# A two-layer decoder trunk: the last layer's output projection with tokens on the partitions, and four output tiles side by side at the start of each layer

## The chip, the cores and the metric

The kernel runs on one core of one Trainium2 chip, as a single program. The metric is the device time of one execution in microseconds (us), inputs and weights in HBM at its start and the output in HBM at its end. A core has a matrix engine (PE, with its weight loads shown apart as PEld), a vector engine (DVE), a scalar engine (ACT), GpSimd (POOL) and a queue engine that starts the transfers (SP). Each works through its own list of instructions in order and waits on semaphores for the others.

## The reference

```python
D_MODEL, SEQ, DEPTH = 1024, 256, 2      # BATCH = 1
N_HEADS, HEAD_DIM, IDX_HEADS, IDX_DIM, D_RNN = 8, 128, 16, 64, 1408
def rmsnorm(x, g):
    return x * rsqrt(mean(x * x, -1, keepdims=True) + 1e-6) * g
for l in range(DEPTH):
    h = rmsnorm(x, norm_g[l])
    q, k, v, ga, iq, ik, iw, xr, gr, ma, mb = split(h @ w_in[l])
    q, k, iq, ik = rope(q), rope(k), rope(iq), rope(ik)
    # index score I[t,s] = sum_h iw[t,h] relu(iq[t,h] . ik[s]); each query keeps its top 64 causal keys
    attn = softmax_attention(q, k, v, kept_keys)
    y_a = (attn * silu(ga)) @ w_out_attn[l]
    xr = causal_depthwise_conv(xr, conv_w[l], conv_b[l])
    y_b = (rg_lru(xr, ...) * silu(gr)) @ w_out_rnn[l]
    x = x + (sigmoid(ma) * y_a + sigmoid(mb) * y_b) @ w_o[l]
return rmsnorm(x, final_g)              # (1, 256, 1024), float32
```

## The kernel before, in words

Activations lie with features on the partitions: the residual stream x is eight tiles of 128 features x 256 tokens. All large matrix products run on PE in fp32r as three products of a high and a low part (`mm3`: high weights by high input, low by high, high by low), so each 128x128 block of weights costs three matmuls.

The weights come from HBM as one stream, `wst`, in the order of use, in chunks of eight blocks (128x1024, 512 KB). A chunk lands in one of four `raw` buffers; ACT (or DVE) copies it to `wh`, the high part, and DVE subtracts to get `wl`, the low part; there are six buffers of each. The first two chunks come in quarters instead (`raq`, 128x256, split into `wq`), so that PE can begin earlier.

`plan()` lists each layer's units in PE's order: `ik` (the index keys and head weights, one output tile `pk`, line 822), `iq` 0 to 7 (index queries, line 853), between them and after them the gates `ga`, `ma`, `mb`, the recurrent branch (`xr`, `gr`, `gate`, whose tiles are `rps` in the profile), then q, k, v and attention, `yb`, `ya` (the two branches' projections, with tokens on the partitions and 512-column matmuls, `by_token`, line 924) and `wo` (line 1156), which turns back to features on the partitions: 128x256 tiles `ops`, added to x.

Work on `ik` and `iq` does not wait for the norm: it multiplies `xg` = x times the gain (line 781, ACT for the high part, DVE for the low), and the factor R = 1/rms per token enters later, in `ci` and `si` (the rotary tables times R), in `iwt`, and in `hf` = x times gain times R (line 851), which is split into `hh` and `hl` for all other projections. `hl` is what the first `ga` matmul needs; `kh` and `kl`, the split rotated index keys, are what the index scores `dots` need.

The norm (lines 709 to 774) has three modes. "wide" (layer 0) multiplies each of eight squared tiles `nsq` with a matrix of ones on PE, at full width 128x256 and in fp32, then takes square root (ACT) and reciprocal (DVE) at 128x256. "added" (layer 1) adds the squares on DVE and needs two narrow sums (one column of output each), square root and reciprocal at 128x2, then two small matmuls `rps` (diagonal `dg` by ones) that spread R over the partitions. "columns" (after the last layer) sums each of the eight squared tiles by two narrow matmuls.

After the last layer (lines 1194 to 1203) the norm is finished, `fo` = x times the final gain (ACT), times R (DVE), and five transfers of 128 or 256 KB write the output, features on the partitions.

The order on each engine is not the order of the code. The class `Program` records every operation with a cost, its inputs and outputs and, for PE, its place in plan order (a `late` term moves it back); then it hands out buffers and picks, engine by engine, what can start earliest. PSUM has four banks with the tag `pp` (pk, iq, ga, ma, mb, ops, ...), two `pq` and two `pt` (norm sums, transposes).

Of the kernel before, what the change touches and what calls it, by code (L numbers as in the profile page):

```python
# [42 lines left out]
for _n, _w in (("g", 8 * L), ("cw", 4 * KR * L), ("cb", KR * L), ("br", KR * L), ("bi", KR * L), ("lam", KR * L),  # L43
               ("fg", 8), ("inv_a", 1), ("sgn_a", 1), ("inv_i", 1), ("sgn_i", 1)):
    PC[_n] = _c
    _c += _w
NPAR = _c

# [16 lines left out]
def plan():  # L65

    u = [("ik",)]
# [4 lines left out]
    u += iq[:NRAW]  # L72
# [19 lines left out]
    u += [("yb", n) for n in range(2)]  # L92
    u += [("ya", n) for n in range(2)]
    u += [("wo", m, 0, 4) for m in range(6)] + [("wo", m, 4, 8) for m in range(6)]
    u += [("wo", m, 0, 8) for m in range(6, 8)]
    return u
# [22 lines left out]
def unit_blocks(u):  # L119

    n = u[0]
    if n == "ik":
        return [("in80", k, OFF["ik"]) for k in range(KD)]
    if n == "attn":
        return []
# [12 lines left out]
    if n == "ya":  # L138
        return [("oa", k, u[1] * 512 + a * P) for k in range(KD) for a in range(4)]
    return [("o", k, u[1] * P) for k in range(u[2], u[3])]  # L140


NBLK = L * sum(len(unit_blocks(u)) for u in plan())
# [3 lines left out]
class H:  # L147


    def __init__(self, pool, tag, shape, dt, name, bufs):  # L150
        self.pool, self.tag, self.shape, self.dt, self.name, self.bufs = pool, tag, shape, dt, name, bufs
        self.tile = None
        self.writer = None
        self.readers = []
        self.users = 0
        self.index = None
# [71 lines left out]
class Program:  # L228
# [15 lines left out]
    def op(self, eng, cost, outs, ins, emit, tabs=ANY, alt=None):  # L244
# [12 lines left out]
        for h in ins:  # L257
            if h.writer is not None and h not in outs:
                o.preds.add(h.writer)
        for h in outs:  # L260
            if h.writer is None:
# [5 lines left out]
            else:  # L267
                o.preds.add(h.writer)
# [4 lines left out]
        for h in outs:  # L273
            h.writer = o.no
            h.readers = []
# [153 lines left out]
def trunk(ctx, tc, xT, pos, par, wst, out):  # L429
# [83 lines left out]
    def load(o, src, cost):  # L513
        pg.op("dma", cost, [o], [], lambda: nc.sync.dma_start(real(o), src))
# [8 lines left out]
    class Stream:  # L523
# [6 lines left out]
        def load(self, upto):  # L530
            while self.nload < min(upto, NCH):
                c = self.nload
                self.nload += 1
                if c < QUARTERS:
                    self.raws[c] = []
                    for i in range(4):
                        raw = f1("raq")
                        load(raw, wst[c][:, 256 * i:256 * i + 256], 400)
# [8 lines left out]
        def chunk(self, c):  # L547
            if c not in self.parts:
# [4 lines left out]
                if c < QUARTERS:  # L553
                    self.parts[c] = []
                    for q in raw:
                        t = halves(r2("wq"))
# [12 lines left out]
        def block(self, n=1):  # L569
# [4 lines left out]
            if c < QUARTERS:  # L574
                s = slice(r % 2 * P, r % 2 * P + P)
                return p[r // 2][0][:, s], p[r // 2][1][:, s]
# [18 lines left out]
    head = const("head", [NPAR + T])  # L595
    load(head, par, 500)
    prm = head[:, :NPAR]
    x = [const(f"x{k}", [T]) for k in range(KD)]
    first = ws.load(QUARTERS)
    for k in range(KD):  # L600
        if k % 2 == 0:
            next(first)
        if k > 0:
            load(x[k], xT[:, k, :], 400)
    for _ in first:
        pass
    pg.after = POS_AFTER
    posi = const("posi", [T], I32)
    load(posi, pos, 400)
    load(x[0], xT[:, 0, :], 400)  # L610
    pg.after = 0.0

    def pc(n, i=0):
        return prm[:, PC[n] + i:PC[n] + i + 1]
# [4 lines left out]
    vset(hpi, math.pi / 2)  # L619
    ones = const("ones", [P])  # L620
# [68 lines left out]
    def decay():  # L689
        lam = prm[:, PC["lam"]:PC["lam"] + NL]  # L690
# [18 lines left out]
    class Norm:  # L709


        def __init__(self, mode):
            self.mode = mode
            self.acc = None
            self.n = 0

        def sums(self, s, first, last):

            if first:
                self.ps = bank("pt", "nps")  # L720
            pg.late = LATE_SUM
            for t in range(2):
                mm(self.ps[:, 0, t:t + 1], s[:, t * P:t * P + P], ones[:, 0:1], first and t == 0, last, True, cost=213)
            pg.late = 0.0

        def all_sums(self, s, first, last):

            if first:
                self.ps = bank("pt", "nps")
            pg.late = LATE_SUM  # L730
            mm(self.ps[:, 0, :], ones, s, first, last, cost=432)
            pg.late = 0.0

        def add(self, k):
            s, xk = f1("nsq"), x[k]
            if self.mode != "added":
                pg.op("act", 94 + 0.833 * T, [s], [xk],
                      lambda: nc.scalar.activation(real(s), real(xk), AF.Square),
                      alt=(67 + 1.046 * T, lambda: nc.vector.tensor_tensor(real(s), real(xk), real(xk), op=OP.mult)))
                if self.mode == "wide":  # L740
                    self.all_sums(s, self.n == 0, self.n == KD - 1)
                else:
                    self.sums(s, self.n == 0, self.n == KD - 1)
            else:
                act(s, xk, AF.Square)
                if self.acc is None:
                    self.acc = s
                else:
                    add(self.acc, self.acc, s)
            self.n += 1  # L750

        def finish(self, copied=True):
            if self.mode == "wide":
# [540 lines left out]
```

## Time and profile before

| | us |
|---|---|
| time, median of 3 runs (lowest, highest) | 711.24 (711.12, 711.37) |
| the profiled execution | 711.33 |
| its span | 709.6 |
| PE busy | 693.7 (98%) |
| DVE busy | 598.0 (84%) |
| ACT busy | 488.8 (69%) |

The profile shows one execution of 711.33 us; its rows lie within the span of 709.6 us, so 1.7 us lie outside of it. Busy time counts an engine's executing instructions; matmuls are pipelined, so a row's mean duration of one matmul is longer than the distance at which they follow each other, and it is the distance that counts for a sum. The chain of waits is the sequence of pieces of work that ended last, followed back from the end.

### The profile page before, as it was taken

Reading aid. Unit: us, or ns where it says so; the run is one execution under the profiler, and the core shown is the slowest. Engines: PE = TensorE matmul, PEld = TensorE weight load, DVE = VectorE, ACT = ScalarE, POOL = GpSimd, SP = SyncE. Lnnn points to the kernel's source line nnn. Section 1 sums busy time; section 2 is a strip of 40 time slices with the busy share of each in tenths; the row PEclk is TensorE's granted clock in tenths of the full one; section 3 lists DMA queues with packets and bytes.
Section 4 is the critical chain, followed back from the end, with each engine's and each line's share of the span. In section 5 each row is a group of like instructions: output and inputs, shape, how many; then the busy total and the mean of one; then the engine's idle time right before and its main releaser. Section 6 shows DMA issues by size and latency. Waiting matters only on the chain.

```text
span 709.6 us, 12900 instructions
## 1 busy us (share of the span) xinstructions
PE 693.7 (98%) x4836; PEld 647.9 (91%) x4836; DVE 598.0 (84%) x1178; ACT 488.8 (69%) x794; POOL 6.4 (1%) x18
## 2 busy tenths in 40 slices
PE   7999999999999999999999999999999999999995
PEld 6988999999999998888999899999999898988895
DVE  6989999899897959857779997999979896996652
ACT  7997675899995748434679776588779674754432
POOL 0000000000000000000000000000000000000000
PEclk9999999999999999999999999999999999999998
DMA  7646556666656452655553555566656545445501
GB/s 256 209 156 209 170 191 203 200 196 217 216 175 194 149 189 76 208 179 178 178 178 113 185 184 186 176 218 207 222 198 194 184 160 176 141 146 174 184 1 61
DMA packets 39402, 124.87 MB, mean 176 GB/s; under 512 B 5036, under 2 KB 9708, under 8 KB 39340
## 3 DMA queue, kind: packets, MB, share of 16 engines
q1 hardware_dynamic: 39340, 124.05, 53.5%
q8 instruction: 38, 0.62, 0.3%
q14 instruction: 24, 0.20, 0.1%
HBM read 119.38 MB, written 1.05 MB: 170 GB/s over the span
## 4 chain that ended last, share of the span: by engine, by line
PE 82%; DVE 8%; ACT 6%; issue 2%; DMA 1%; SPq 0%; DVEq 0%; ACTq 0%
PE rps L508 15%; PE yb L508 9%; PE ops L508 7%; PE k L508 6%; PE q L508 6%; PE ma L508 6%; PE v L508 6%; PE ya L508 6%; PE gps L508 5%; PE mb L508 4%; PE ga L508 4%; DVE wl L482 2%; ACT wh L476 2%; PE lg L508 2%; PE av L508 2%
## 5 line engine op out<-in xcount | busy, mean ns | idle before, releaser
L482 DVE TENSOR_TENSOR wl<-raw,wh 128x1024 fp32r<-128x1024 f32 x223 | 271.5, 1219 | 62.6 <-ACT wh L476 61.3
L476 ACT ACTIVATE wh<-raw 128x1024 fp32r<-128x1024 f32 x199 | 210.4, 1058 | 135.8 <-PE ya L508 22.9
L508 PE MATMUL rps<-hl,wh 128*128 128x256 f32 x352 | 99.6, 283 | 0.0
L508 PE MATMUL rps<-hh,wl 128*128 128x256 f32 x352 | 99.6, 283 | 0.0
L508 PE MATMUL rps<-hh,wh 128*128 128x256 f32 x352 | 99.6, 283 | 0.0
L508 PEld LDWEIGHTS rps<-hh,wh 128*128 128x128 f32 x352 | 67.5, 192 | 0.2
L508 PEld LDWEIGHTS rps<-hh,wl 128*128 128x128 f32 x352 | 67.5, 192 | 0.2
L508 PEld LDWEIGHTS rps<-hl,wh 128*128 128x128 f32 x352 | 67.5, 192 | 0.0
L508 PE MATMUL yb<-wh,g 128*128 128x512 f32 x176 | 58.9, 396 | 0.0
L508 PE MATMUL iq<-xg,wh 128*128 128x256 f32 x240 | 44.7, 284 | 0.0
L508 PE MATMUL ya<-wh,aT 128*128 128x512 f32 x128 | 40.3, 393 | 0.0
L508 PEld LDWEIGHTS iq<-xg,wh 128*128 128x128 f32 x240 | 37.9, 192 | 0.0
L508 PEld LDWEIGHTS yb<-wh,g 128*128 128x128 f32 x176 | 32.5, 188 | 5.3
L508 PE MATMUL ga<-hl,wh 128*128 128x256 f32 x128 | 36.3, 284 | 0.7 <-DVE hl L482 0.7
L508 PE MATMUL ops<-ml,wh 128*128 128x256 f32 x128 | 36.8, 287 | 0.0
L508 PE MATMUL ops<-mh,wl 128*128 128x256 f32 x128 | 36.7, 287 | 0.0
L508 PE MATMUL ops<-mh,wh 128*128 128x256 f32 x128 | 36.6, 286 | 0.0
L508 PE MATMUL q<-hh,wl 128*128 128x256 f32 x128 | 36.4, 284 | 0.0
L508 PE MATMUL q<-hh,wh 128*128 128x256 f32 x128 | 36.3, 284 | 0.0
L508 PE MATMUL k<-hh,wl 128*128 128x256 f32 x128 | 36.3, 284 | 0.0
L508 PE MATMUL q<-hl,wh 128*128 128x256 f32 x128 | 36.2, 283 | 0.0
L508 PE MATMUL k<-hh,wh 128*128 128x256 f32 x128 | 36.2, 283 | 0.0
(232 smaller groups left out, 1980.4 us busy)
## 6 DMA issues: line engine op xcount, KB each, us to landing
raw<-in_wst_dram SPq DMA_DIRECT2D x223, 512.0 KB, 3.5
xk<-xs SPq DMA_DIRECT2D x24, 48.0 KB, 3.7
raq<-in_wst_dram SPq DMA_DIRECT2D x8, 128.0 KB
x<-in_xT_dram SPq DMA_DIRECT2D x8, 128.0 KB, 3.4
out_dram<-fo SPq DMA_DIRECT2D x3, 256.0 KB
xk<-xs SPq DMA_DIRECT2D x8, 40.0 KB
xf<-xs SPq DMA_DIRECT2D x2, 160.0 KB
xf<-xs SPq DMA_DIRECT2D x2, 144.0 KB
```

Source lines behind the costliest of these rows:

```text
L476: lambda: nc.scalar.activation(real(o), real(i), AF.Copy),
L482: lambda: nc.vector.tensor_tensor(real(o), real(a), real(b), op=op))
L508: lambda: nc.tensor.matmul(real(o), real(w), real(m), start=start, stop=stop, skip_group_check=grp))
```

## The change

It has four parts.

1. Loads. The parameters are split: the norm gains, the rotary constants and the first x tile come first (`pre`, 128x276 and x 128x256), the rest (`prm`) after the first weights. x comes in pairs of tiles (`xp`). The first two chunks of weights come in four halves (`rah`, 128x512, split into `whh` and `whl`) instead of eight quarters, with whole chunks (`raw`) between them. A one-column sine loads ACT's table at the start.
2. The start of a layer. The unit `head` replaces `ik` and `iq` 0 to 2: for each of the eight rows of weights it runs the three matmuls of four output tiles (pk, iq 0, 1 and 2), in three PSUM banks.
3. The norm. There is one mode for both layers: squares of a pair of tiles (128x512) on ACT or DVE, added on DVE, then four narrow sums, square root and reciprocal of 128x2, two `dg` and two `rps`, and an ACT copy of R. x is updated in pairs of tiles.
4. The end of the last layer. `xt` transposes x to tokens on the partitions (16 transposes on PE, 4 copies on ACT) and loads the final gain, repeated on all partitions. `wt` replaces `wo`: 96 matmuls of 128x512 instead of 192 of 128x256, tokens on the partitions; the second half of the features finishes token tile 0 first and then token tile 1. The sum of squares of a token is then along the row: ACT's Square with an accumulated output. Square root and reciprocal are 128x1, and ACT scales the first half of a row, DVE the second. Four transfers of 256 KB write the output.

```diff
-    u = [("ik",)]
+    u = [("head",)]
-    u += iq[:NRAW]
+    u += iq[3:NRAW]
     u += [("yb", n) for n in range(2)]
+    if l == L - 1:
+        return u + [("xt", 0), ("ya", 0), ("xt", 1), ("ya", 1), ("wt", 0), ("wt", 1)]
...
     class Norm:
+        def add(self, i):
+            s = f2("nsq")
+            square(s.join(), xp[i].join())          # ACT, or DVE where that is earlier
+            if self.acc is None:
+                self.acc = s
+            else:
+                add(self.acc, self.acc, s)
+        def sums(self, s):
+            self.ps = bank("pt", "nps")
             pg.late = LATE_SUM
             for t in range(2):
-                mm(self.ps[:, 0, t:t + 1], s[:, t * P:t * P + P], ones[:, 0:1], first and t == 0, last, True, cost=213)
+                for a in range(2):
+                    mm(self.ps[:, 0, t:t + 1], s[:, a, t * P:t * P + P], ones[:, 0:1], t == a == 0, a == 1, True, cost=213)
-        def all_sums(self, s, first, last):
-            mm(self.ps[:, 0, :], ones, s, first, last, cost=432)
...
-        def ik(self):
-            pk = bank("pp", "pk")
+        def head(self):
+            pk, one, two = bank("pp", "pk"), bank("pp", "iq"), bank("pp", "iq")
             ps = pk[:, 0, :]
-            proj(ps, self.xg)
             self.R = R = self.norm.finish()
+            for k in range(KD):
+                for n, o in enumerate((ps, one[:, 0, :], one[:, 1, :], two[:, 0, :])):
+                    mm3(o, self.xg[k], k == 0 and n != 2, k == KD - 1, True)
...
+        def xt(self, n):
+            for t in range(2):
+                bk = bank("pt", "xps").join()
+                for c in range(4):
+                    trans(bk[:, c * P:c * P + P], x[4 * n + c][:, t * P:t * P + P])
+                self.turned[n, t] = r2f("xt").join()
+                act(self.turned[n, t], bk, AF.Copy)
+        def wt(self, n):
+            ps = self.by_token("ops", self.m, True, True, n == 1)
+            for t in range(2):
+                y, z = self.turned[n, t], r2f("z").join()
+                add(y, y, ps[t])
+                ss = const(f"ss{n}{t}", [1])
+                act(f2("sq").join(), y, AF.Square, accum_out=ss)
+                mul(z, y, self.fg[n])
+                if n == 0:
+                    tsc(ss, ss, 1.0 / D, EPS, OP.mult, OP.add)
+                else:
+                    act(ss, ss, AF.Sqrt, scale=1.0 / D, bias=self.ss[t])
+                    recip(ss, ss)
+                    act(o, o, AF.Copy, scale=ss)
+                    tsc(z, z, ss, None, OP.mult)
+                    ...
-    R = norm.finish(False)
-    for w in (1, 2, 2, 2, 1):
-        act(o[:, a, :], x[n + a], AF.Copy, scale=pc("fg", n + a))
-        mul(o, o, R.twice()[:, :w, :])
```

Three places show how the instructions stand. On PE, the start of the program, before (pk is the index key tile, iq the index queries, nps the norm's sums):

```order
L508 MATMUL nps35_114<-nsq34_107,ones21_83 128x256
L508 MATMUL pk64_130<-xg33_105,wq65_111 128x256 x3
L508 MATMUL pk64_130<-xg36_118,wq65_111 128x256 x3
L508 MATMUL nps35_114<-nsq37_135,ones21_83 128x256
L508 MATMUL pk64_130<-xg38_123,wq66_128 128x256 x3
L508 MATMUL nps35_114<-nsq39_147,ones21_83 128x256
L508 MATMUL pk64_130<-xg40_141,wq66_128 128x256 x3
```

The same place after:

```order
L512 MATMUL pk54_120<-xg28_108,whh63_102 128x256
L512 MATMUL pk54_120<-xg28_108,whl64_106 128x256
L512 MATMUL pk54_120<-xg28_108,whh63_102 128x256
L512 MATMUL iq55_128<-xg28_108,whh63_102 128x256
L512 MATMUL iq55_128<-xg28_108,whl64_106 128x256
L512 MATMUL iq55_128<-xg28_108,whh63_102 128x256 x2
L512 MATMUL iq55_128<-xg28_108,whl64_106 128x256
L512 MATMUL iq55_128<-xg28_108,whh63_102 128x256
L512 MATMUL iq56_139<-xg28_108,whh63_102 128x256
```

Each tile of xg is now used for twelve matmuls at once rather than three, and the wide sums are gone from between them.

On ACT, around the norm of layer 0, before (sd is the square root, raw the landed chunks):

```order
L469 ACTIVATE sd69_275<-nps35_114,epst19_74 128x256
L476 ACTIVATE wh114_295<-raw113_228 128x1024
L679 ACT_TABLE_LOAD
L679 ACTIVATE stab_i28_309<-ang51_171,head1_72 128x256
L680 ACTIVATE ctab_i27_311<-kk52_181,hpi20_81 128x256
L476 ACTIVATE wh130_335<-raw129_251 128x1024
```

And after (rstd is R, rps the tile from which it is copied):

```order
L473 ACTIVATE sd58_290<-nps57_273,epst13_81 128x2
L473 ACTIVATE sw79_310<-pk54_120 32x256
L480 ACTIVATE wh141_314<-raw140_267 128x1024
L473 ACTIVATE sw79_310<-pk54_120 32x256
L473 ACTIVATE sw94_330<-iq55_128 32x512
L480 ACTIVATE wh145_343<-raw144_285 128x1024
L473 ACTIVATE rstd62_354<-rps59_346 128x256
```

R now comes by way of PE and ACT, and two copies of whole chunks stand between the square root and it.

On DVE, the end of the program, before (x is the residual stream, fo the output):

```order
L482 TENSOR_TENSOR x79_145<-x79_145,ops1544_8562 128x256
L504 RECIPROCAL sd1550_8608<-sd1550_8608 128x2
L497 TENSOR_SCALAR dg1552_8611<-ident22_76,sd1550_8608 128x128
L497 TENSOR_SCALAR dg1553_8613<-ident22_76,sd1550_8608 128x128
L482 TENSOR_TENSOR fo1554_8467<-fo1554_8467,rps1551_8615 128x256
L482 TENSOR_TENSOR fo1555_8476<-fo1555_8476,rps1551_8615 128x512
L482 TENSOR_TENSOR fo1556_8509<-fo1556_8509,rps1551_8615 128x512
L482 TENSOR_TENSOR fo1557_8543<-fo1557_8543,rps1551_8615 128x512
L482 TENSOR_TENSOR fo1558_8603<-fo1558_8603,rps1551_8615 128x256
```

And after (xt is x turned to tokens on the partitions, z the row times the gain, ss the sum of squares; the first four rows belong to token tile 0, the last four to tile 1):

```order
L486 TENSOR_TENSOR xt1484_8281<-xt1484_8281,ops1529_8366 128x512
L486 TENSOR_TENSOR z1543_8451<-xt1484_8281,fg1487_8307 128x512
L508 RECIPROCAL ss101544_8449<-ss101544_8449 128x1
L501 TENSOR_SCALAR z1543_8451<-z1543_8451,ss101544_8449 128x512
L486 TENSOR_TENSOR xt1486_8296<-xt1486_8296,ops1530_8441 128x512
L486 TENSOR_TENSOR z1546_8482<-xt1486_8296,fg1487_8307 128x512
L508 RECIPROCAL ss111547_8480<-ss111547_8480 128x1
L501 TENSOR_SCALAR z1546_8482<-z1546_8482,ss111547_8480 128x512
```

Behind the last addition there are now a product, a reciprocal and one scaling on DVE, where two `dg` and five products stood, and no matmul is between them.

## Rows read from the trace of the kernel before

**Rows 1.** The page: busy time of each engine, and the chain by engine.

```profile
PE 693.7 (98%) x4836; PEld 647.9 (91%) x4836; DVE 598.0 (84%) x1178; ACT 488.8 (69%) x794; POOL 6.4 (1%) x18
...
PE 82%; DVE 8%; ACT 6%; issue 2%; DMA 1%; SPq 0%; DVEq 0%; ACTq 0%
```

**Rows 2.** Windows: length, busy PE, PEld, DVE, ACT, POOL, clock, DMA share, GB/s.

```profile
0.00:20.00 20.00, 15.67 (x85) 13.84 (x86) 12.59 (x33) 14.75 (x31) 1.29 (x10) 1.00 0.76 253
20.00:60.00 40.00, 37.00 (x281) 34.75 (x280) 37.04 (x54) 38.49 (x55) 0.00 (x0) 1.00 0.54 174
60.00:100.00 40.00, 39.68 (x306) 38.16 (x306) 39.70 (x90) 27.62 (x47) 0.00 (x0) 1.00 0.63 206
100.00:330.00 230.00, 230.00 (x1530) 211.80 (x1529) 197.47 (x412) 162.44 (x265) 2.49 (x4) 1.00 0.56 183
```

**Rows 3.** Timeline of the start: start, length, engine, what; idle before it in brackets.

```profile
3.42 0.51 ACT L781 ACTIVATE xg<-head 128x256 fp32r<-128x256 f32 x1 [1.40 <-DMA head<-in_par_dram]
...
13.70 0.59 PE L508 MATMUL nps<-nsq,ones 128*128 128x256 f32 x2
...
14.48 0.59 PE L508 MATMUL nps<-nsq,ones 128*128 128x256 f32 x2
...
17.58 0.28 PE L508 MATMUL iq<-xg,wh 128*128 128x256 f32 x1
```

**Rows 4.** The chain in order of time: start, us, what (four pieces).

```profile
61.29 5.77 PE rps L508 x48
...
309.80 16.32 PE ya L508 x72
...
326.47 0.33 PE mps L511 x3
...
694.07 0.12 PE nps L508 x2
```

**Rows 5.** Timeline of DVE: R, and the last kl of layer 0.

```profile
19.55 1.75 DVE L504 RECIPROCAL rstd<-sd 128x256 f32<-128x256 f32 x1 [0.56 <-ACT sd L469]
...
57.14 0.42 DVE L482 TENSOR_TENSOR kl<-ikr,kh 64x256 fp32r<-64x256 f32 x1
```

**Rows 6.** Groups of DVE and ACT: busy us, mean ns of one, idle before.

```profile
L482 DVE TENSOR_TENSOR wl<-raw,wh 128x1024 fp32r<-128x1024 f32 x223 | 271.5, 1219 | 62.6 <-ACT wh L476 61.3
...
L497 DVE TENSOR_SCALAR lt<-lt,mx 128x256 f32<-128x256 f32 x16 | 5.5, 346 | 0.0
...
L497 DVE TENSOR_SCALAR lt<-lt,mx 128x128 f32<-128x128 f32 x16 | 4.4, 278 | 0.0
L482 DVE TENSOR_TENSOR wq<-raq,wq 128x256 fp32r<-128x256 f32 x8 | 3.3, 422 | 1.9 <-ACT wq L476 1.9
...
L482 DVE TENSOR_TENSOR fo<-fo,rps 128x512 f32<-128x512 f32 x3 | 1.9, 680 | 0.0
...
L469 ACT ACTIVATION_READ_ACCUMULATOR lt<-lt,mx 128x1 f32 x32 | 6.0, 188 | 0.0
...
L476 ACT ACTIVATE hh<-hf 128x512 fp32r<-128x512 f32 x8 | 4.8, 618 | 0.0
```

**Rows 7.** Wait of PE: total us, times, longest.

```profile
PE dots L508 <- ACT kh L476: 0.9, 1, 0.9
```

**Rows 8.** Timeline of the end.

```profile
699.43 0.36 PE L508 MATMUL ops<-ml,wh 128*128 128x256 f32 x1
...
699.84 0.42 DVE L482 TENSOR_TENSOR x<-x,ops 128x256 f32<-128x256 f32 x1 [3.34 <-PE ops L508]
...
701.51 0.26 ACT L469 ACTIVATE sd<-nps,epst 128x2 f32<-128x2 f32 x1 [0.41 <-PE nps L508]
701.81 0.17 DVE L504 RECIPROCAL sd<-sd 128x2 f32<-128x2 f32 x1 [1.55 <-ACT sd L469]
...
703.66 2.63 SPq L1202 DMA_DIRECT2D out_dram<-fo  x5
```

**Rows 9.** DMA from 700 to 709.6 us: GB/s in 40 slices of 0.24 us.

```profile
GB/s 0 0 0 0 0 0 0 0 0 0 0 0 0 0 0 0 0 0 47 350 150 282 367 393 384 384 384 359 410 346 337 179 0 0 0 0 0 0 34 0
```

More of the change, by code (lines that the diff above doesn't have):

```diff
@@ L121, in unit_blocks @@
     n = u[0]
-    if n == "ik":
-        return [("in80", k, OFF["ik"]) for k in range(KD)]
-    if n == "attn":
+    if n == "head":
+        return [b for k in range(KD)
+                for b in [("in80", k, OFF["ik"])] + [("in", k, OFF["iq"] + i * P) for i in range(3)]]
+    if n in ("attn", "xt"):
         return []
@@ L139, in unit_blocks @@
         return [("oa", k, u[1] * 512 + a * P) for k in range(KD) for a in range(4)]
+    if n == "wt":
+        return [("o", k, u[1] * 512 + a * P) for k in range(KD) for a in range(4)]
     return [("o", k, u[1] * P) for k in range(u[2], u[3])]
-NBLK = L * sum(len(unit_blocks(u)) for u in plan())
+NBLK = sum(len(unit_blocks(u)) for l in range(L) for u in plan(l))
 NCH = -(-NBLK // 8)
@@ L266, in op @@
                 lst.append(h)
-            else:
-                o.preds.add(h.writer)
+            elif not beside:
+                o.preds.update(h.writers)
             o.preds.update(h.readers)
@@ L594, in trunk @@
     ws = Stream()
[L595 to L601, printed above, removed]
+    prm = const("prm", [NPAR - NPRE])
+    head = const("head", [NPRE + 2 * T])
+    xp = [head[:, NPRE:].split(2)] + [const(f"xp{i}", [2, T]) for i in range(1, KD // 2)]
+    x = [xp[k // 2][:, k % 2, :] for k in range(KD)]
+    posi = const("posi", [T], I32)
+    first = ws.load(KD // 2)
+    load(head[:, :NPRE + T], pre, 400)
+    next(first)
+    load(x[1], xT[:, 1, :], 400, True)
+    pg.shift = -9000.0
+    load(posi, pos, 400)
+    pg.shift = 0.0
+    next(first)
+    for i in range(1, KD // 2):
+        load(xp[i], xT[:, 2 * i:2 * i + 2, :], 800)
+        next(first)
+        if i < HALVED:
             next(first)
-        if k > 0:
-            load(x[k], xT[:, k, :], 400)
     for _ in first:
         pass
[L607 to L611, printed above, removed]
+    load(prm, par, 400)
     def pc(n, i=0):
-        return prm[:, PC[n] + i:PC[n] + i + 1]
+        i += PC[n]
+        return head[:, i:i + 1] if i < NPRE else prm[:, i - NPRE:i - NPRE + 1]
     epst = const("epst", [1])
@@ L709, in trunk, with __init__, square @@
     class Norm:
-        def __init__(self, mode):
-            self.mode = mode
+        def __init__(self):
             self.acc = None
[L715 to L720, printed above, removed]
+        def add(self, i):
+            def square(o, a):
+                n = o.size()
+                pg.op("act", 94 + 0.833 * n, [o], [a],
+                      lambda: nc.scalar.activation(real(o), real(a), AF.Square),
+                      alt=(67 + 1.046 * n, lambda: nc.vector.tensor_tensor(real(o), real(a), real(a), op=OP.mult)))
+            s = f2("nsq")
[4 more added lines that the diff above has]
+                add(self.acc, self.acc, s)
@@ L734, in add @@
[L734 to L750, printed above, removed]
@@ L844, in ik @@
                 self.make_h(k)
+            self.banks["iq"] = one
+            self.queries(1)
+            self.banks["iq"] = two
         def make_h(self, k):
@@ L1176, in trunk @@
+    norm = Norm()
     xg = []
-    kept = x[0]
-    x[0] = head[:, NPAR:]
     for k in range(KD):
         xg.append(scaled(0, k))
-        norm.add(k)
-    x[0] = kept
+        if k % 2:
+            norm.add(k // 2)
     tables()
@@ L1215 @@
 LEAD = 2000.0
-MODES = ("wide",) + ("added",) * (L - 1) + ("columns",)
 AFTER = 20000.0
-POS_AFTER = 3000.0
 LATE_SUM = 10000.0
```

167 lines of the change are left out of this document (83 added, 84 removed).

## The prediction

> **What bounds the kernel now.** I read the busy times and the chain first. PE is busy for 693.7 of 709.6 us and holds 82% of the chain [rows 1]; the reader is to see that only two things can shorten this kernel: fewer or cheaper matmuls, and less of the some 16 us in which PE stands. The windows then show where it stands. From 100 us on it is full (230.00 of 230.00 to 330), while it misses 4.33 us in the first 20, 3.00 in the next 40 and 0.32 in the 40 behind those [rows 2]. The rest is the end: from the start of the last output matmul at 699.43 to 709.6 there are 10.17 us with hardly a matmul of use [rows 8].
>
> The same windows tell who makes PE wait. In 20 to 60 us ACT is busy for 38.49 of 40 and DVE for 37.04, in 60 to 100 DVE for 39.70 [rows 2]. So early matmuls that finish sooner do not by themselves make the program shorter: what decides is when DVE and ACT hand over `hl` and `kl`. The last `kl` of layer 0 ends at 57.56 [rows 5], the first `dots` waits for it.
>
> **The start.** Eight wide sums go: from one sum to the next there are 0.78 us, with three pk matmuls of 0.12 between them (48 `rps` take 5.77), so one costs 0.42 and eight 3.4 [rows 3, 4]. Four narrow sums of 0.12 [rows 4] and two `rps`, about 0.4 together as an estimate, come in: 2.5 us less PE work. That helps only where PE is late, so I count it through the times at which things are ready.
>
> Before, the 96 matmuls of pk and iq 0 to 2 are through at about 23.2: at 17.58 the last 48 have begun, 0.12 each, and only one of them is done [rows 3, 4]. After, the rows of weights come as halves with whole chunks and pairs of x between; by my count 3.2 MB have to land before the last of the eight rows can be split, which at the mean of 253 GB/s [rows 2] is 12.7 us. ACT then owes two `xg` copies and the chunk copies ahead of them, DVE two subtractions: about 17 us, and the last two rows' 24 matmuls bring PE to some 19.2. The lower end is 16.1 (a start at 4.6, then 96 times 0.12), the upper the old 23.2. Taken: 4.0 us of lead.
>
> Does it last until `dots`? PE finds more to do there: nine more `rps` matmuls (0.12) and eight more `mb` of 512 columns (16.32/72 = 0.227 [rows 4]) stand ahead of the first `dots`, 2.9 us of work done earlier. DVE has more ahead of the last `kl`, by counting its order: two more `wl` (a row of 1.22, 1.14 back to back), two casts taken over from ACT (1.0 together, an estimate: one operand less than a `wl`), and for the rest four half subtractions, three pair sums, two `dg` (4.9 us by the rows of 512 and 128 columns) in place of eight quarter subtractions, two squares and the wide reciprocal (8 and 2 times 0.34, and 1.75) [rows 5, 6]: 3.1 us more. ACT has 1.0 less.
>
> Before, DVE idles for 7.41 us to 20 and 2.96 from there to 60 [rows 2]: 10.4, of which 3.4 stand before any data is there [rows 3], 7.0 behind. If all of it stays, `kl` is 3.1 later, at 60.7; if nothing behind the first data stays, at 53.7. Walking down DVE's and ACT's new order with these durations and landings I come to 55.3, with the idle time of 20 to 60 us almost gone because ACT, which held DVE there, has less to do; a walk sees too few waits, and half of the 7.0 kept gives 57.2. I take 56.2. PE itself, with its lead, would be there at 54.4 (57.6 less 4.0 and the 3.0 of idle time, plus the 2.9 and 0.9 of new work), so it waits 1.8. The gain at this point is 57.6 - 56.2 + 2.9 = **4.3 us**. Its ends: -0.2 with `kl` at 60.7, and 6.1 with PE never waiting.
>
> **The layer boundary.** Two more narrow sums, 0.24 [rows 4]; squares of pairs and `x` sums of pairs of 0.68 instead of two of 0.42 are off PE. Twelve matmuls for a row of weights now need each `xg` later than before, and `dots` of layer 1 comes some 3 us later in PE's order, while two more `wl` stand ahead of its `kl`. Today's wait for `kh` is 0.9 [rows 7]. I take 0.3 lost; the ends are 0.9 gained (the wait gone) and 1.3 lost.
>
> **The last layer's matmuls.** 192 of 128x256 at 0.12 are 23.1 us, 96 of 128x512 at 0.227 are 21.8 [rows 4]: 1.3 gained. Eight narrow sums that stand among the last output matmuls go (0.12 each, 1.0), and 16 transposes come (0.33 for three, 1.8) [rows 4]. Together 0.5; their copies on ACT, 4 of 0.62, and the 512 KB of gains lie beside `ya`, with DVE and ACT under half busy there, and the first half's additions and squares beside the second half's 5.4 us for token tile 1. Say 0.6 with ends 0.2 and 1.0.
>
> Here a rule of the Trainium skill would say otherwise. The row gives 0.227 for a 512-column matmul in this kernel's own fp32r form. "TensorE: Matmul & The Clock Gate", section "Back-to-back issue gap", gives about 131 ns as the sustained distance at 512 columns, and 216 ns for the isolated gap (109 at 256). By the first, an estimate, the 96 would take 12.6 us and the time would be about 694.5; by the second the swap gains 0.2 instead of 1.3. The row agrees with neither exactly and is far from the first, so the row decides; I leave the page's first figure a chance of 0.01.
>
> **The end.** Before: 10.17 us from the start of the last `ops` matmul, of which the addition begins 0.41 later, the square root ends at 701.77, the output starts at 703.66 [rows 8] and moves until about 707.7 at some 385 GB/s, then 1.9 us of closing [rows 9]. After: a 512-column matmul is 0.11 longer, so the addition begins at 0.52 and takes 0.68; Square 0.62 and its accumulator 0.19 bring 2.0; square root 0.26 to 2.3, reciprocal 0.17 to 2.5 [rows 6, 8]. DVE's scaling of 128x512 is no row of before: 0.28 at 128 and 0.35 at 256 columns point to 0.48 as an estimate; the ends are 0.28 and the 0.68 of a two-input form. ACT's scaling, 0.62 to 0.72, runs beside it. First output issued at 3.0, data 0.7 later as before, 512 KB at 385 GB/s are 1.4 us, so 5.1 to 5.3, and 1.9 to close: 7.1. Token tile 0's two transfers are out of the way by then. **3.0 gained**, ends 2.3 and 3.5. The product with the gain (0.68) hides beside Square.
>
> **Sum.** 4.3 - 0.3 + 0.6 + 3.0 = 7.6, so 711.33 - 7.6 = **703.7 us** (the profiled run is 0.09 over the median).
>
> **Rivals.** *DVE sets the pace and the lead is not kept*: it is 99% busy in 60 to 100 us, and the change adds to its work ahead of `kl`. Then the front gives -0.2 to 2, and with 3.3 from elsewhere the time is 706 to 708.2. *PE never waits again*: 6.1 in front, 9.4 in all, 701.9, or 700.5 with the good ends of the other terms; against it speaks that ACT and DVE are nearly full there. *Slower*: R is late. It used to come straight from DVE at 21.3 [rows 5]; now it passes PE twice and ACT, where two copies of whole chunks stand ahead of the copy of R, each waiting for a transfer. I put R at 22.5. Each microsecond beyond that moves `hf`, `hl` and `kl` one for one; from 9 us (R past 31.5) the whole gain is eaten, and at 12 the time is 715.7. For it speaks the order; against it that at 253 GB/s those chunks, the tenth and eleventh of half a megabyte, are in by 21 us, so it would need chunks held back by full buffers.
>
> **How the numbers follow.** Forecast 0.60 (702.5 to 706), lead not kept 0.20, PE never waiting 0.15, late R 0.03, and 0.02 for what lies outside of these. The range is 700.6 to 707.6: it takes in most of both neighbours. What a measurement of this kernel can tell from no change is about 0.2%, 1.4 us. Lead not kept together with the bad ends of the boundary and of the end comes to 710.2, which is within that bound: faster 0.94, within 0.03, slower 0.03.
>
> **What would show it.** Right: matmuls of `head` done near 19 us; the copy of R near 22.5; the last `kl` of layer 0 near 56 and PE's idle time of 20 to 60 us under 3; `ops` at 0.227 apart; about 7.1 us from the last `ops` matmul to the end. Wrong: `kl` at 59 or later, DVE full from 10 to 100 us and PE waiting for `hl` and `dots` by 4 us or more; new waits at the start of layer 1 beyond 2 us; `ops` at another distance; or an output that starts later than 3.5 us behind the last matmul.

## The result and the profile after

The changed kernel takes 706.62 us (median of 4 runs, 706.28 to 706.97) against 711.23 us before (4 runs): a ratio of 0.9935, 95% interval 0.9918 to 0.9952. That is 4.6 us less, where 7.6 were forecast; the time lies in the stated range. A second measurement of the same kernel on another chip gave the same ratio (0.9935, 0.9923 to 0.9948). The profiled execution took 706.28 us with a span of 704.5; it is the fastest of the four, so its rows add up to a little more gain (5.1) than the medians (4.6).

The page of the changed kernel, busy times and the chain by engine:

```profile
PE 687.6 (98%) x4720; PEld 638.4 (91%) x4720; DVE 602.8 (86%) x1179; ACT 478.0 (68%) x771; POOL 6.5 (1%) x18
...
PE 88%; ACT 5%; DVE 3%; issue 2%; DMA 1%; SPq 0%; DVEq 0%
```

PE is busy 6.1 us less and the span is 5.1 shorter, so PE stands 1.0 longer than before [rows 1]. That is a sum of stages that went opposite ways: 2.1 more in the first 100 us, 0.35 more at the start of layer 1 (330 to 410 us), and 1.4 less behind the last output matmul (7.4 of 10.17 us before, 6.1 of 6.46 now). The windows of the changed kernel (columns as in [rows 2]) show the first part:

```profile
0.00:20.00 20.00, 13.30 (x87) 12.10 (x88) 13.08 (x26) 14.47 (x23) 1.28 (x10) 1.00 0.81 275
20.00:60.00 40.00, 37.50 (x282) 35.24 (x282) 36.57 (x60) 36.48 (x54) 0.00 (x0) 1.00 0.51 161
60.00:100.00 40.00, 39.49 (x303) 37.98 (x304) 39.81 (x83) 28.23 (x49) 1.22 (x1) 1.00 0.63 205
100.00:330.00 230.00, 230.00 (x1526) 211.58 (x1525) 199.67 (x424) 157.34 (x258) 1.43 (x3) 1.00 0.56 183
```

In the first 100 us PE is busy for 90.29 instead of 92.35 [rows 2], so it stands 2.1 longer there. How far ahead it is can be read from the first matmul of a stage that both kernels have. Before, the first q of layer 0, the first pk of layer 1, the first q of layer 1 and the first ops of layer 1:

```profile
197.23 0.28 PE L508 MATMUL q<-hh,wh 128*128 128x256 f32 x1
...
356.22 0.28 PE L508 MATMUL pk<-xg,wh 128*128 128x256 f32 x1
...
538.94 0.28 PE L508 MATMUL q<-hh,wh 128*128 128x256 f32 x1
...
673.96 0.28 PE L508 MATMUL ops<-mh,wh 128*128 128x256 f32 x1
```

The same four in the changed kernel, the last `ops`, and the end:

```profile
196.20 0.28 PE L512 MATMUL q<-hh,wh 128*128 128x256 f32 x1
...
355.21 0.28 PE L512 MATMUL pk<-xg,wh 128*128 128x256 f32 x1
...
538.65 0.28 PE L512 MATMUL q<-hh,wh 128*128 128x256 f32 x1
...
675.58 0.39 PE L512 MATMUL ops<-wh,mh 128*128 128x512 f32 x1
...
698.04 0.39 PE L512 MATMUL ops<-wh,ml 128*128 128x512 f32 x1
698.47 0.69 DVE L486 TENSOR_TENSOR xt<-xt,ops 128x512 f32<-128x512 f32 x1 [2.95 <-PE ops L512]
...
699.73 0.19 ACT L473 ACTIVATION_READ_ACCUMULATOR sq<-xt 128x1 f32 x1
...
700.47 0.49 DVE L501 TENSOR_SCALAR z<-z,ss 128x512 f32<-128x512 f32 x1
700.98 0.81 SPq L1213 DMA_DIRECT2D out_dram<-z  x2
```

From these rows the ledger of this execution is: the start and layer 0 give 1.03 us (197.23 to 196.20), the start of layer 1 takes 0.73 back (only 0.29 ahead at its q), the last layer's matmuls bring the lead to 1.39 at the last `ops` (699.43 in [rows 8], 698.04 here), and from there to the end 6.46 us pass instead of 10.17, which gives 3.7. Together 5.1, the difference of the spans.

What PE waited for in the changed kernel (us in all, times, longest):

```profile
PE pk L512 <- ACT xg L771: 4.8, 1, 4.8
PE mb L512 <- DVE ga L486: 1.3, 1, 1.3
PE dots L512 <- ACT rl L473: 1.1, 1, 1.1
PE pk L512 <- DVE whl L486: 0.9, 1, 0.9
PE dots L512 <- DVE kl L486: 0.8, 1, 0.8
PE pk L512 <- ACT whh L480: 0.8, 1, 0.8
PE ga L512 <- DVE iwt L486: 0.5, 1, 0.5
PE ga L512 <- ACT hh L480: 0.3, 1, 0.3
```

Two of the longer ones are new: PE stands 0.8 and 0.9 at the fourth row of weights (`whh`, `whl`). The wait at `mb`, whose PSUM bank comes free only when DVE has multiplied the first `ga` tile, has grown to 1.3; before it was

```profile
PE mb L508 <- DVE ga L482: 0.4, 1, 0.4
```

R and `kl`, which [rows 5] showed before, now:

```profile
24.63 0.38 ACT L473 ACTIVATE rstd<-rps 128x256 f32<-128x256 f32 x1
```

```profile
60.03 0.42 DVE L486 TENSOR_TENSOR kl<-ikr,kh 64x256 fp32r<-64x256 f32 x1
```

R is there at 25.0 and the last `kl` at 60.45, that is 3.7 and 2.9 us later than before.

### The profile page after: what moved, and what is told of

It reads as the page before. It is cut to its first block, busy times and chain, and to the rows that moved or that the text cites. A ratio compares the mean times of both kernels' runs of the same rounds, so it can differ in the third digit from the quotient of the medians.

```text
span 704.5 us, 12625 instructions
## 1 busy us (share of the span) xinstructions
PE 687.6 (98%) x4720; PEld 638.4 (91%) x4720; DVE 602.8 (86%) x1179; ACT 478.0 (68%) x771; POOL 6.5 (1%) x18
## 4 chain that ended last, share of the span: by engine, by line
PE 88%; ACT 5%; DVE 3%; issue 2%; DMA 1%; SPq 0%; DVEq 0%
PE rps L512 16%; PE yb L512 9%; PE q L512 7%; PE k L512 7%; PE ops L512 6%; PE ma L512 6%; PE ya L512 6%; PE v L512 6%; PE ga L512 6%; PE mb L512 5%; PE gps L512 5%; PE iq L512 3%; PE dots L512 2%; PE lg L512 2%; PE av L512 2%
## 5 line engine op out<-in xcount | busy, mean ns | idle before, releaser
L480 ACT ACTIVATE wh<-raw 128x1024 fp32r<-128x1024 f32 x195 | 206.2, 1058 | 142.5 <-PE rps L512 21.9
L512 PE MATMUL ga<-hh,wh 128*128 128x256 f32 x128 | 36.4, 284 | 0.8 <-DVE iwt L486 0.5
L512 PE MATMUL k<-hl,wh 128*128 128x256 f32 x128 | 36.2, 283 | 0.0
L512 PE MATMUL ga<-hh,wl 128*128 128x256 f32 x128 | 36.2, 283 | 0.0
```

The costliest lines, as they stand in the source:

```text
L480: lambda: nc.scalar.activation(real(o), real(i), AF.Copy),
L512: lambda: nc.tensor.matmul(real(o), real(w), real(m), start=start, stop=stop, skip_group_check=grp))
```

## The experiments

Twelve kernels were run, each beside the kernel before on the same chip. "Below before" is always against that, and is worked out from the ratio; the difference of the two medians can be some tenths away from it. The changed kernel stands 4.6 below.

**The end alone (tail_only).** The kernel before, with `xt`, `wt` and the outputs of the changed one:

```diff
+    if l == L - 1:
+        return u + [("xt", 0), ("ya", 0), ("xt", 1), ("ya", 1), ("wt", 0), ("wt", 1)]
-    R = norm.finish(False)
-    ...
```

> Before's start, norm and layer boundary, with the changed end of the last layer alone (transposes, 512-column matmuls, token-major norm, four 256 KB transfers). Theory (the end and the last layer's matmuls carry nearly all of the gain, and do so whatever the start is): last ops matmul 1.1 us earlier than in before against the start of ya, 6.5 us from its start to the end of the span instead of 10.2, so 711.2 - 1.1 - 3.7 = 706.4. Rival (the head is worth 2 us or more, and the boundary or the end gives it back): about 4.6 - 2 = 2.6 us of gain, 708.6.

707.42 against 711.7, ratio 0.9943 (0.9931 to 0.9956): 4.1 below before. The last `ops` matmul starts at 698.40 and the span ends at 705.4, 7.0 later. So the end and the last layer's matmuls carry 4.1 of the gain of 4.6 with nothing of the new start, as the theory had it, although the time is 1.0 above the theory's 706.4. All of the new loads, the head and the norm are left with about half a microsecond, which is not clear of the two intervals. And as much stands behind the last matmul: 7.0 us here, 6.46 in the changed kernel, though both write the output alike (first output issued 2.95 and 2.94 behind the last matmul). The DMA from 695.8 us on, in 40 slices of 0.24 us, shows where, with its queues below it:

```profile
GB/s 0 0 0 9 350 375 410 376 393 273 0 0 0 0 0 0 0 0 0 0 0 0 0 0 0 0 154 358 393 376 401 393 111 0 0 0 0 0 34 0
...
q14 instruction: 1, 0.01, 0.3%
```

One packet of an instruction queue lands behind the output's data, and the span ends some 1.7 us after these. The kernel before has such a packet at its end too (the 34 in [rows 9]); the changed kernel has none.

**R early (sums_early).**

```diff
-LATE_SUM = 10000.0
+LATE_SUM = 0.0
```

> The changed kernel with the norm's narrow sums and rps at their place in plan order instead of 10 us later, so that R of layer 0 is ready some 4 to 6 us earlier; kl stands at the same place in DVE's order (rows 85 and 87). Theory 1 (kl of layer 0 is late because DVE and ACT have as much to do ahead of it as they can): kl ends at 60.5 within 1 us and the time is 706.6 within 0.7. Theory 2 (kl is late because R comes at 25.0 instead of 21.3): kl ends 3 us or more earlier, about 57, and the time is about 704.

710.28, ratio 0.9989 (0.9980 to 0.9999): 3.7 worse than the changed kernel; both numbers missed. The edit moved more than the sums: x was loaded ahead of the weights, and the first matmul starts at 9.52 instead of 4.84. What it does show is in two rows, ACT's copy of R and then DVE's last `kl`:

```profile
18.78 0.38 ACT L473 ACTIVATE rstd<-rps 128x256 f32<-128x256 f32 x1 [3.63 <-PE rps L512]
```

```profile
61.73 0.42 DVE L486 TENSOR_TENSOR kl<-ikr,kh 64x256 fp32r<-64x256 f32 x1
```

R came 5.9 us earlier and `kl` 1.7 later. R is not what holds `kl` here. As PE was later too, the run says nothing more.

**The keys first (kl_first).**

```diff
+            pg.shift = -KL_FIRST          # 10000.0, around rotate, kh and kl
             rotate(ikr[:64], ps[:64], f1("sw")[:64], [t[:64] for t in self.ti], 32)
```

> The changed kernel with the rotary chain and the split of the index keys raised in the scheduler's order: the second kl stands at row 77 of DVE instead of 87, in front of four whole-chunk subtractions, with the same work in all. Theory 1a (only the place of kl in the order makes PE wait, DVE has slack behind it): kl some 6 us earlier, PE's wait of 1.0 at 59.5 goes, and dots start earlier: 705.0 to 705.8. Theory 1b (DVE's total work up to about 120 us is the limit, whatever stands first): what is moved back is waited for instead, PE's idle time of 50 to 100 us stays within 0.5 of its 2.7: 706.6 within 0.5.

707.06, ratio 0.9946 (0.9928 to 0.9964): no gain over the changed kernel. In the profile `kl` of layer 0 ends at 49.8 instead of 60.45 and q of layer 0 starts at 195.18, 1.0 earlier:

```profile
49.34 0.42 DVE L486 TENSOR_TENSOR kl<-ikr,kh 64x256 fp32r<-64x256 f32 x1
```

```profile
195.18 0.28 PE L512 MATMUL q<-hh,wh 128*128 128x256 f32 x1
```

In this execution the last `pk` already starts 0.35 earlier (20.53 for 20.88), so 10.7 us off `kl` are worth some 0.7 at q. The edit acts in layer 1 too, where it gave more than this back: PE waited twice for `dots` (2.6 us in all), and behind that the granted clock fell:

```profile
400.00:405.00 5.00, 3.16 (x25) 2.75 (x23) 4.42 (x8) 2.21 (x3) 0.00 (x0) 1.00 0.88 320
405.00:410.00 5.00, 4.28 (x20) 4.29 (x21) 4.22 (x9) 2.36 (x7) 0.00 (x0) 0.51 0.75 229
410.00:415.00 5.00, 5.00 (x30) 4.73 (x30) 3.10 (x6) 2.57 (x5) 0.00 (x0) 0.81 0.31 110
```

In 405 to 410 us the clock is at 0.51, that is at 1.2 GHz nearly throughout. The profiled execution took 709.81 us, the three others 706.89 to 707.18, so this doesn't happen in each of them.

**DVE relieved by GpSimd (pool_ang).**

```diff
-            tsc(ang, posf, pc("inv_" + n), None, OP.mult)
+            tsc(ang, posf, pc("inv_" + n), None, OP.mult, eng="pool" if n == "i" else "dve")
             ...                          # the other steps of the angles likewise
```

> The changed kernel with the angles of the index keys' rotary tables (one cast, three scalar steps, four multiply-adds, one clamp) on GpSimd instead of DVE: DVE has about 3.2 us less ahead of kl, the sine table's values are made ahead of the square root, so ACT has one table load (1.28) less ahead of kh. Theory 1 (DVE's and ACT's work ahead of kl sets the start): kl 2.5 to 3.5 us earlier than 60.5 and PE's position at q of layer 0 earlier by 1.5 to 3: 703.6 to 705.1. Theory 2 (R decides): R moves by less than 1 us, kl within 1 us of 60.5, 706.6 within 0.6. Against theory 1 counts too if GpSimd's work slows DVE's instructions (a wl row of 1.22 longer by more than a tenth).

707.61, ratio 0.9946 (0.9932 to 0.9960): no gain, `kl` at 59.9, only 0.6 earlier. It doesn't tell the theories apart, since GpSimd's work made DVE's longer. Two of DVE's rows beside it:

```profile
12.01 1.71 DVE L486 TENSOR_TENSOR wl<-raw,wh 128x1024 fp32r<-128x1024 f32 x1
...
15.72 1.23 DVE L486 TENSOR_TENSOR nsq<-nsq,nsq 128x512 f32<-128x512 f32 x1
```

A `wl` subtraction took 1.71 instead of 1.22, a sum of 512 columns 1.23 instead of 0.68. GpSimd's last step ends at 17.2 us, and `wl` at 22.59 takes 1.23 again. The head's last `pk` also starts 0.7 later here (21.54).

**More and less work on DVE (dve_extra, dve_less).**

```diff
                 sub(wl, raw, wh.bitcast(F32))
+                if c in EXTRA:                 # (4, 5)
+                    sub(wl, raw, wh.bitcast(F32))
```

> The changed kernel with two of layer 0's early whole-chunk subtractions (chunks 4 and 5) done twice: 2.3 us more work on DVE before 35 us, one more subtraction in the count ahead of kl (18 for 17), nothing else added. Theory 1 (DVE's work up to about 100 us is what PE waits for): q of layer 0 begins 1.1 to 2.3 us later than 196.2 and the time is only 2.3 to 3.5 us below before. Rival (DVE has slack, ACT or R decides): q within 0.4 of 196.2, time 4.2 to 4.6 below before.

```diff
+                if c in LESS:                  # (8, 10, 12, 14)
+                    wl = self.last
+                else:
+                    sub(wl, raw, wh.bitcast(F32))
+                self.last = wl
```

> The changed kernel without four of layer 0's whole-chunk subtractions (chunks 8, 10, 12 and 14 use the low part of the chunk before them, so these low parts are not the ones of the reference): 4.6 us less work on DVE, 12 subtractions instead of 17 ahead of the last kl, all matmuls as they were. Theory 1 (DVE's work up to about 100 us is what PE waits for): kl of layer 0 two to four us earlier than 60.5, PE's waits of 30 to 63 us under 3 instead of 4.5, q of layer 0 at 193.5 to 195, 5.8 to 7.3 us below before. Rival (ACT, R or the landing of the weights decides): q within 0.5 of 196.2, 4.1 to 5.1 below before.

With 2.3 us more work, q of layer 0 starts at 197.38, 1.2 later than in the changed kernel's profile (theory 1's lower end); the time is 707.35, ratio 0.9941 (0.9928 to 0.9953), 4.2 below before, which is the rival's number. So about half of the added work reaches PE in this execution, the longest of the five, and less of it the median. With 4.6 us less work, the kernel is slower: 708.18, ratio 0.9954 (0.9941 to 0.9966). Theory 1 falls in the form I gave it. `kl` did come 5.8 us earlier (54.7), but the order that the scheduler made of the smaller work put something else late: DVE's rotary product `iqr`, which frees the bank that `mb` needs. PE's wait:

```profile
PE mb L512 <- DVE iqr L486: 3.3, 1, 3.3
```

And the clock behind it:

```profile
50.00:54.00 4.00, 0.99 (x6) 0.51 (x4) 3.68 (x7) 3.88 (x8) 0.00 (x0) 1.00 0.71 210
54.00:58.00 4.00, 3.70 (x9) 2.99 (x10) 3.94 (x7) 3.89 (x5) 0.00 (x0) 0.57 0.39 114
```

So what PE waits for at 50 to 63 us is not set by the sum of DVE's work alone. These two runs and kl_first fit another reading, that the places of three handovers in DVE's order count (the product that frees a bank for `mb`, `ga` or `iqr`; the two `kl`); work put ahead of them in the same order is then passed on in part, as in dve_extra.

**The fourth half first (half_first).**

```diff
-                        load(raw, wst[c][:, 512 * i:512 * i + 512], 800)
+                        pg.shift = -HALF_FIRST * (c == i == 1)        # 3500.0, and the same for its split
+                        load(raw, wst[c][:, 512 * i:512 * i + 512], 800)
```

> The changed kernel with the fourth half of the first weights loaded and split ahead of the first whole chunk, so that PE no longer stands 0.9 and 1.1 us at the fourth row of weights (11.8 to 14.3). Theory 1 (the first dots wait for kl, so an earlier head is given back): the last pk matmul 1 to 2 us earlier than 20.9, kl of layer 0 still at 60.5 within 0.7, PE's waits from 30 to 63 us longer by about as much, time within 0.5 of the changed kernel's (4.6 us less than before). Rival (a lead at the head is kept to the end of the layer): q of layer 0 begins 1.5 us earlier than 196.2, and the time is 6 us or more below before.

705.85, ratio 0.9919 (0.9905 to 0.9933): 5.8 below before, between the two numbers. The last `pk` starts at 19.66 instead of 20.88 and q of layer 0 at 195.41, 0.8 earlier: about two thirds of the 1.2 us is kept. What was given back stands at `mb`, as before:

```profile
PE mb L512 <- DVE ga L486: 2.0, 1, 2.0
```

Behind this wait the granted clock was 0.74 in 54 to 58 us, 1.00 in the changed kernel.

**Layer 1 in the old order (old_layer1).**

```diff
-    u = [("head",)]
+    u = [("head",)] if l == 0 else [("ik",)]
-    u += iq[3:NRAW]
+    u += iq[3 if l == 0 else 0:NRAW]
```

> The changed kernel with layer 1 begun in the old order (one tile of index keys, then the queries one after the other) and layer 0 as changed. Theory 1 (the 0.7 us lost between the end of layer 0 and q of layer 1 are the four tiles side by side, whose dots and kl stand behind two more subtractions): the loss goes, q of layer 1 begins 1.0 us earlier than in before, not 0.3, and the time is 5.2 us below before. Rival (the loss comes from the norm by pairs or from DVE's backlog): the loss stays within 0.3, 4.6 below before.

705.92, ratio 0.9925 (0.9913 to 0.9938): 5.3 below before. From the first pk of layer 1 to its first q 182.92 us pass (356.51 to 539.43), 182.72 in the kernel before and 183.44 in the changed one. So 0.5 of the 0.7 lost there is the order of four tiles at once; combo and combo_ga, with the old order too, show 182.98 and 183.03, after_again 183.47; the medians' own difference, 0.7, is not clear of its interval.

**The same kernel again (after_again).**

> The changed kernel once more, beside the runs of this call. Both theories: 4.6 us below before, within 0.6; the copy gives the spread from chip to chip.

706.9 against 711.58, ratio 0.9935: as before. Its five runs were 706.28, 706.36, 706.90, 707.41 and 707.85, and the profile is that of the longest. It shows where they differ. The window 16 to 18 us, first in this execution:

```profile
14.00:16.00 2.00, 2.00 (x13) 2.00 (x14) 2.00 (x4) 2.00 (x5) 0.00 (x0) 0.75 1.03 392
16.00:18.00 2.00, 2.00 (x11) 2.00 (x11) 2.00 (x5) 1.98 (x3) 0.00 (x0) 0.50 0.70 214
18.00:20.00 2.00, 2.00 (x18) 2.00 (x17) 2.00 (x3) 1.16 (x1) 0.00 (x0) 0.90 0.62 221
```

and in the execution profiled first:

```profile
14.00:16.00 2.00, 1.73 (x14) 1.73 (x15) 2.00 (x5) 2.00 (x4) 0.00 (x0) 1.00 1.04 388
16.00:18.00 2.00, 2.00 (x19) 2.00 (x18) 2.00 (x4) 2.00 (x3) 0.00 (x0) 1.00 0.69 229
```

Ahead of it, both executions have PE standing 0.8 and 0.9 us at the fourth row of weights. In one the clock is granted in full afterwards, in the other it is at 0.50 for some 3 us, 11 matmuls begin in 2 us instead of 19, and the last `pk` starts at 22.08 instead of 20.88: 1.2 us, which the span has too (705.7 to 704.5). The profiles of old_layer1 and not_apart, which begin like the changed kernel, show the same 0.50 in 16 to 18 us, and their last `pk` starts at 22.22 and 22.30. In such an execution nothing of the lead at q of layer 0 is left (197.23 before):

```profile
197.32 0.28 PE L512 MATMUL q<-hh,wh 128*128 128x256 f32 x1
```

That half_first, which takes these two waits away, has runs within 0.6 us of each other fits, but wasn't tested further.

**Three edits, and four (combo, combo_ga).** The first joins half_first, kl_first in layer 0 alone and old_layer1. The second adds:

```diff
+                pg.shift = -GA_FIRST if self.l == 0 and i == 1 else 0.0        # 25000.0
                 act(t, bk, AF.Sigmoid)
                 mul(t, t, bk)
+                pg.shift = 0.0
```

> The changed kernel with three edits: the fourth half first, the index keys' chain of layer 0 ahead of four subtractions on DVE, and layer 1 begun in the old order. Theory 1 (kl's place is worth the 1.0 us of waiting at 59.5, the order of layer 1 its 0.7, the earlier half nothing by itself but up to 1.5 once kl is early): 6.3 to 7.5 us below before, q of layer 0 at 193.5 to 195.2. Rival (DVE is full up to 120 us and only its work counts): 4.3 to 5.2 below before.

> The three edits together (fourth half first, keys of layer 0 early on DVE, layer 1 begun in the old order), and with them the sigmoid and the product of the first ga tile raised on ACT and DVE, so that its PSUM bank comes free before PE's mb needs it. Theory 1 (in the three edits together the wait that is left in 50 to 63 us is mb for this bank, 1.9 us): that wait goes, q of layer 0 about 1.5 us earlier than with the three edits, 7 to 8 us below before. Rival (DVE is full to 120 us, so what is raised only puts off something else): another wait of 1 us or more in its place, 6 to 6.8 below before.

The three edits give 705.32, ratio 0.9909 (0.9895 to 0.9922): 6.5 below before, near theory 1's lower end. But q of layer 0 starts at 196.03, no earlier than in the changed kernel: with `kl` at 49.1 PE waits 1.9 us for `ga`'s bank. With that raised too the time is 704.34, ratio 0.9899 (0.9884 to 0.9914), 7.2 below before, and q of layer 0 starts at 194.17. The wait at `mb` for `ga` is gone; in its place stands a shorter one, and the rival is half right:

```profile
PE rps L514 <- DVE iqr L488: 1.5, 1, 1.5
...
PE mb L514 <- DVE wl L488: 0.7, 1, 0.7
```

This version beats both kernels: beside the changed kernel on the same chip 704.34 (704.04 to 704.50) against 706.90 (706.28 to 707.85). By themselves half_first gave 1.2 of these 2.6 us, old_layer1 0.7 and kl_first nothing; what the three make together, and `ga` on top, was not taken apart further.

**Both token tiles together (not_apart).**

```diff
-            ps = self.by_token("ops", self.m, True, True, n == 1)
+            ps = self.by_token("ops", self.m, True, True, False)
```

> The changed kernel with the last half of the output matmuls going to both token tiles alternately, so that both end together, instead of tile 0 first. Theory (tile 0's addition, norm, scaling and half of the output lie under tile 1's 5.4 us of matmuls): now two additions, two products and two Squares stand behind the last matmul (0.6 us more on DVE for the addition, 0.8 on ACT, 0.6 for the second scaling) and 1 MB instead of 0.5 is to be written (1.4 us more): 8.5 to 9.5 us from the last matmul's start to the end instead of 6.5, 2.0 to 3.0 us more than the changed kernel. Rival (the output's end is set by the last tile's chain alone): under 1 us more.

708.12, ratio 0.9951 (0.9939 to 0.9964): 1.2 more than the changed kernel, between the two numbers. From the last `ops` (699.34) to the end (707.2) it is 7.86 us, 1.4 more. The first output is issued as soon after the last matmul as before:

```profile
702.28 1.81 SPq L1213 DMA_DIRECT2D out_dram<-z  x4
```

702.28 is 2.94 behind the last matmul's start, and so is 700.98 in the changed kernel. The second tile's additions and scalings hide behind the first's; only the second half megabyte (1.4 us) is seen. That is what finishing tile 0 first is worth.

## Why the forecast was right in direction and too large

**The front failed at two steps**, and the larger is the first: "Taken: 4.0 us of lead." The lead was 1.3. Counted as the forecast does, by the 96 matmuls of pk and iq 0 to 2, the last of them starts at 23.22 before and at 21.96 after (nine iq matmuls of the last row follow the last `pk` of 20.88). First before, then after, with the first matmul of the fifth row of weights; a line marked x2 holds that matmul and the next:

```profile
23.22 0.40 PE L508 MATMUL iq<-xg,wh 128*128 128x256 f32 x2
```

```profile
15.44 0.28 PE L512 MATMUL pk<-xg,wh 128*128 128x256 f32 x1
...
21.96 0.40 PE L512 MATMUL iq<-xg,wh 128*128 128x256 f32 x2
```

The forecast let the landing of the last row set the end of the head ("about 17 us"). The first rows set it: the 48 matmuls of rows 1 to 4 took from 4.84 to 15.44, 10.6 us where 0.12 each makes 5.8, and from there to the end of the head PE did not stand any more. The first matmul starts 0.95 later than before (the first wide sum at 3.89), the first row's matmuls stand 0.21 apart, and PE waits at the fourth row, where a whole chunk is loaded, copied and subtracted ahead of the half that PE needs next; half_first takes that wait away and the head ends 1.2 earlier. The eight wide sums took 3.5 us in all, near the 3.4 forecast, though not at my 0.42 each: 0.5 to 0.65 for the first four, as long as PE's matmuls stood 0.21 apart, 0.24 for the next three (pk follows at 13.94 the one that starts at 13.70 [rows 3]) and 0.5 for the last.

The second step is "I take 56.2" for `kl`, which ended at 60.45. DVE had been busy for 50.07 us up to there, 47.22 up to 57.56 before, so it had idled for 10.4 us both times. "If all of it stays, `kl` is 3.1 later, at 60.7" was the end of the range that came true: the added work, 2.9, was counted nearly rightly, the hope that idle time would go was not borne out.

Of the missing 3.3 us (1.03 at q of layer 0, 4.3 forecast) the lead accounts for most, by two readings. In kl_first `kl` came at 49.8, earlier than any forecast, and q was still only 2.05 ahead of before. And with a lead of 1.3 instead of 4.0, and the 2.5 us that PE still stood in 20 to 60 us, the forecast's own sum has PE at the `dots` at 59.6 instead of 54.4, whatever `kl` does, and so a gain of 57.6 - 59.6 + 2.9 = 0.9.

So the time came out in the band of "lead not kept" (706 to 708.2), but not for its reason. There was little lead to keep, and 1.03 of the 1.3 was kept. From the last `pk` to q of layer 0 there are 175.2 to 175.4 us in after, after_again, old_layer1, not_apart, sums_early and pool_ang, with the last `pk` anywhere from 20.88 to 24.33: what the head loses is passed on in full. DVE's total work, the rival's reason, was not the whole limit either, as dve_less shows.

That the time lies in the range is in part luck. The front and the boundary together gave 3.7 less than forecast, the last layer and the end 1.2 more; without these 1.2 the time would be 707.8, just outside. One sum of the forecast is also off: "700.5 with the good ends of the other terms" comes to 699.8 by its own ends (6.1 + 0.9 + 1.0 + 3.5 from 711.33).

**The layer boundary** cost 0.73 where I took 0.3, inside its bounds; old_layer1 gives back 0.5 of it.

**The last layer's matmuls** gave 1.1 (a lead of 0.29 at q of layer 1, 1.39 at the last `ops`), where I took 0.6 with an end of 1.0. The distance of 512-column matmuls was right:

```profile
691.86 6.59 PE ops L512 x29
```

6.59 us for 29 are 0.227 each, the row of `ya` [rows 4]. "TensorE: Matmul & The Clock Gate" of the Trainium skill ("Back-to-back issue gap") would have them follow each other at 131 ns; the trace does not show it here, and its 216 ns for an isolated matmul is the nearer figure. The other half microsecond is the narrow sums. Between the first and the last `ops` 25.47 us passed before. 191 distances of 0.12 are 22.9 of them, and the eight transposes `mps` that stand among them took 0.9, then as now; this leaves about 1.6 for the eight sums, 0.2 each, where 0.12 was taken. (The time from q to the first `ops` grew by 1.9, near the 1.8 taken for 16 transposes.)

**The end** gave 3.7 where 3.0 were forecast, just past the end of 3.5. The chain of arithmetic was right to 0.1 (first output issued 2.94 behind the last matmul, 3.0 forecast; DVE's scaling of 128x512 0.49, 0.48 forecast). The mis-sized term is the closing, the time behind the last data. Here is the DMA rate from 694.9 to 704.5 us, in 40 slices of 0.24 us:

```profile
GB/s 0 0 0 0 0 0 290 341 410 376 401 350 17 0 0 0 0 0 0 0 0 0 0 0 0 0 0 0 60 384 367 367 393 393 222 0 0 0 0 0
```

Data stop at about 703.3, 1.2 us ahead of the end, where [rows 9] left 1.9. The new end is not what shortened it: tail_only has the same end, and its closing is some 1.7 us with the packet of an instruction queue behind the data, so that its end gives 3.2 (10.17 to 7.0), close to the forecast. That this packet is the reason fits both kernels that have it, but no run tests it. Tile 0's two transfers lie under the matmuls (the first burst), as the forecast had it.

**Late R**, the case for slower, was partly there: R came at 25.0, not at 22.5, but sums_early shows that `kl` does not follow it.

## What to carry to other kernels

Count a lead on PE by the same set of matmuls before and after, and look for what sets its end in the first rows as well as in the last: here a loss at the head was passed on in full for 175 us. An engine's idle time ahead of a handover is not a reserve to count on: where the handover's place in that engine's order follows more work than before, it can come later by the whole of that work (2.9 us here; dve_extra's 2.3 us made `kl` 0.9 later), so put that case into the sum, and look for the next handover that PE meets, a PSUM bank as well as an operand, before crediting a lead. When a scheduler makes the order, name the two or three handovers and try them one by one: raising `kl` alone gave nothing in the median, while the load order of the fourth half, `kl`, the bank of `ga` and the old order of layer 1 together gave 2.6 us, more than the whole new start had given. The chain behind the last matmul is the part that can be added up row by row: up to the issue of the output it came out to a tenth of a microsecond, and only the closing behind the data did not.

## What the runs showed of the hardware

Two waits of PE of 0.8 and 0.9 us, at 11.5 to 14 us, were followed in one execution of the same program by some 3 us mostly at 1.2 GHz (granted clock 0.50 in 16 to 18 us) and in another by none: 1.2 us of difference at the last `pk`. In dve_less a wait of 3.3 us at 51 us was followed by a clock of 0.57 over 54 to 58 us, one of 2.0 in half_first by 0.74, one of 1.3 in the changed kernel and one of 1.9 in combo by 1.00. So a wait of PE can cost more than its length, and an early start made of pieces with gaps between them is open to that.

While GpSimd did elementwise work beside DVE (pool_ang, to 17.2 us), single DVE instructions took up to 0.55 us longer (1.71 for 1.22, 1.23 for 0.68), and not afterwards; the 3.2 us taken off DVE brought `kl` forward by only 0.6.
